# A two-layer decoder in fp32: VectorE makes the sums of the weights one item earlier in chunks of seven block products, and the block sums move to other buffers

## The chip, the cores and the metric

The kernel runs on one core of one Trainium2 chip. The metric is the time of one launch on the device in microseconds (us), lower is better. The kernel before was timed three times: 2167.9 us median, 2167.6 lowest, 2168.16 highest.

## What is computed

The reference is a decoder of two layers on 256 tokens of width 2048, all in fp32: a gated token mixer and a convolutional feed-forward part in layer 0, attention with forget gates and the same feed-forward part in layer 1, and a final norm. The change touches only the down projection of the feed-forward part, a product of a 256 x 5632 matrix with a 5632 x 2048 weight, once in each layer:

```python
def conv_ffn(xn, w_up, conv_w, conv_b, w_down):
    S = xn.shape[1]
    h = xn @ w_up
    hp = jnp.pad(h, ((0, 0), (CONV_W - 1, 0), (0, 0)))
    h = sum(hp[:, k:k + S] * conv_w[k] for k in range(CONV_W)) + conv_b
    gate, val = jnp.split(h, 2, axis=-1)
    return (jax.nn.silu(gate) * val) @ w_down
...
for l in range(DEPTH):
    ...
    h = h + conv_ffn(rmsnorm(h, f_norm[l]), f_w_up[l], f_conv_w[l],
                     f_conv_b[l], f_w_down[l])
```

## The kernel before

**Two parts of every number.** Each fp32 operand is split into a rounded part (`hi`, in a buffer `whi`) and a remainder (`lo`, in `wlo`), and TensorE multiplies hi by hi, hi by lo and lo by hi. For weights that arrive from memory, ScalarE (ACT in the profile) rounds (`whi`), and VectorE (DVE) then subtracts to get the remainder (`wlo`). So each piece of the weights costs one instruction on each of the two engines, and then 24 matmuls of 256 columns.

**The stream of items.** All weights pass through one `Stream`. Its items are pieces of 128 x 1024 numbers. At step i, `Stream.run` issues the load of item i + 6 on SyncE's queue (SP), splits item i + 3 into two parts, lets TensorE multiply item i, and then advances every piece of side work that is pending by one `yield`. Each engine works its own list strictly in this order. There are four buffers for loaded pieces (`raw`), four for rounded parts and four for remainders. A load waits until the piece that lay in its buffer has been split, and a rounded part is written once TensorE has done with the item four places back.

**Chunks of seven block products.** In the down projection (`seven_block`) the output is made in blocks of 512 columns: three in layer 0 (its last 512 columns are made in another way), four in layer 1. A block has 22 chunks of the weight. Most are plain, 24 matmuls. The chunks listed in `SUMMED` are done with seven block products instead of eight, from sums of weight blocks and sums of activation blocks. Such a chunk is two items of the stream: the first (`mult_plain`) multiplies three quarters of the loaded weights as they are, 9 matmuls; the second (`mult_sums`) has no load of its own, and multiplies four sums of weight blocks, 12 matmuls. In what follows a plain item is called C, the first item of a chunk of seven A, and the second B. A block runs as a sequence like C A B C A B C C A B. `order_of` sets it: two A B pairs in block 0, eight in the other blocks but the last of layer 1, which has six. Together that is 42 pairs.

**The sums of the weights.** `weight_sums` makes the four sums of a chunk with three additions on VectorE (lines 495, 497, 498). They lie in a buffer called `room`, of which there are two. In the kernel before, they are made when item A is split, so VectorE's list reads: the additions of A, the remainder of A, the remainder of B, the remainder of the next C, and so on. ScalarE rounds B from those sums, and VectorE then makes B's remainder from that.

**Side work.** The sums of the activations for the chunks of seven (`all_sums`, lines 474 to 484) are made at the start of a down projection and use the same two `room` buffers. At the end of a block's chunks of seven, the sums that TensorE has gathered in `m` are added to the result: in layer 1 by `sums_into_residual` (lines 590 to 602), which holds a `room` buffer (`one`) through five steps; in layer 0 by `sums_apart` (lines 611 to 631), which has its own buffer, and then turns each half of the block on VectorE (line 927), sends it to memory in four DMAs on SP's queue (line 934), fetches it back in another layout (line 938), and adds it to `h` (line 642). These DMAs stand in the same queue as the loads of the weights.

Of the kernel before, what the change touches and what calls it, by code (L numbers as in the profile page):

```python
# [14 lines left out]
OP = mybir.AluOpType  # L15
AX = mybir.AxisListType

P = 128
# [26 lines left out]
class Stream:  # L45
# [4 lines left out]
        self.items, self.pending = [], []  # L50
        self.raw, self.parts = {}, {}

    def chunk(self, src, mult, at, at_load=None, at_split=None, rows=(1, 1), place=None, split=None):


        self.items.append((src, mult, at_load, at_split, at, rows, place, split))

    def then(self, at_load=None, at_split=None, at_mult=None):
        self.items.append((None, at_mult, at_load, at_split, 0, None, None, None))

    def start(self, gen):
        self.pending.append(gen)
# [4 lines left out]
                self.pending.remove(g)  # L67

    def _load(self, i):
        src, _, at_load, _, _, _, place, _ = self.items[i]  # L70
        if at_load:
            at_load()
        if src is None:
            return
        if place is None:
            place = self.pool.tile([P, CHUNK], F32, name="raw", tag="raw", bufs=LOADS - AHEAD + 1)
        raw = place[:, :src.shape[1]]
        self.nc.sync.dma_start(raw, src)
        self.raw[i] = raw
# [10 lines left out]
        return hi, lo  # L90

    def _split(self, i):
        if self.items[i][3]:
            self.items[i][3]()
        raw, split = self.raw.pop(i, None), self.items[i][7]
        if split:
            self.parts[i] = split(raw)
            return
        if raw is None:
            return  # L100
        at, (n, pitch) = self.items[i][4:6]
        hi, lo = self.room(at)
        raw = raw.rearrange("p (n w) -> p n w", n=n)
        h, l = hi, lo
        if n > 1:
            h, l = (a[:, :n * pitch].rearrange("p (n w) -> p n w", n=n) for a in (h, l))
        else:
            h, l = h[:, None, :], l[:, None, :]
        h, l = (a[:, :, :raw.shape[2]] for a in (h, l))
        self.nc.scalar.activation(h, raw, AF.Copy)  # L110
        self.nc.vector.tensor_tensor(l, raw, h.bitcast(F32), op=OP.subtract)  # L111
        self.parts[i] = (hi, lo)
# [63 lines left out]
def build(ctx, tc, d, out):  # L176
# [307 lines left out]
        nc.vector.tensor_tensor(lo, f, hi.bitcast(F32), op=OP.subtract)  # L484

    def all_sums():
        for _ in range(4):
            yield
        for q in range(0, len(SUMMED), 2):
            yield from sums_of_blocks(q, SUMMED[q])  # L490
# [10 lines left out]
    def seven_block(blk, src, order, done, sums_done):  # L501
# [50 lines left out]
        def seven(c, i, first):  # L552
            q = SUMMED.index(c)
            sums = block_sums()[:, q]
            own = {}

            def split(raw):
                own["t"] = weight_sums(raw)
                return s.two_parts(raw[:, T:], TOK_AT)

            def mult_plain(hi, lo):
                if first:
                    box["m"] = main_ps()
                m, ps = box["m"], box["ps"]
                three(m[:, 0, :T], (hi, lo), at(2 * c, 0), 0, first, i == lasts)
                three(ps(0, T), (hi, lo), at(2 * c + 1, 0), 2, False, False)
                three(ps(0, 0), (hi, lo), [sums[:, 3, l, :] for l in range(2)], 1, False, False)

            def mult_sums(hi, lo):
                m, ps = box["m"], box["ps"]  # L570
                three(m[:, 1, :T], (hi, lo), [sums[:, 1, l, :] for l in range(2)], 0, first, i == lasts)
                three(m[:, 1, T:], (hi, lo), [sums[:, 0, l, :] for l in range(2)], 1, False, i == lasts)
                three(m[:, 0, T:], (hi, lo), [sums[:, 2, l, :] for l in range(2)], 2, False, i == lasts)
                three(ps(1, T), (hi, lo), at(2 * c + 1, 1), 3, False, False)
                if i == lasts:
                    s.start(sums_done(m))

            s.chunk(src[c], mult_plain, TOK_AT, split=split)
            s.chunk(None, mult_sums, TOK_AT, split=lambda _: s.two_parts(own["t"], TOK_AT))

        for i, (c, s7) in enumerate(order):
# [5 lines left out]
    def sums_into_residual(blk):  # L587

        def done(m):
            hh = by_token()[:, :, blk * 512:(blk + 1) * 512]  # L590
            one = room()[:, :3 * T].rearrange("p (a b) -> p a b", a=3)
            nc.scalar.activation(one[:, 0, :], m[:, 0, :T], AF.Copy)
            yield
            nc.vector.tensor_tensor(one[:, 1, :], one[:, 0, :], m[:, 0, T:], op=OP.add)
            nc.vector.tensor_tensor(one[:, 2, :], one[:, 1, :], m[:, 1, T:], op=OP.subtract)
            yield
            nc.vector.tensor_tensor(hh[:, :, :T], hh[:, :, :T], m[:, 1:, :T].to_broadcast([P, 2, T]), op=OP.add)
            yield
            nc.vector.tensor_tensor(hh[:, :, :T], hh[:, :, :T], one[:, 1:, :], op=OP.subtract)
            yield  # L600
            nc.vector.tensor_tensor(hh[:, :, T:], hh[:, :, T:], one[:, 0::2, :], op=OP.add)
            state["summed"] += 1
        return done

# [273 lines left out]
    def room():  # L878
        return ph.temp("room", [P, CHUNK])
# [419 lines left out]
```

## Time and profile before

| | |
|---|---|
| median of three runs | 2167.9 us |
| the profiled execution, its own time | 2168.81 us |
| its span, first to last instruction | 2167.1 us |
| mean granted TensorE clock | 0.999 |
| VectorE busy in the span | 1619.4 us, 75% |
| ScalarE busy in the span | 1187.0 us, 55% |
| DMA, mean | 208 GB/s |

The profile is of one execution. Its span runs from the first to the last instruction, and its own time is 1.7 us longer than the span. A row of a timeline gives the start in us from the start of the span, the duration in us, the engine, the line, the operation, what it writes and reads, and how many instructions of a kind stand together; in brackets, for how long the engine was idle before, and who ended that wait. In the views of waits the three numbers are us in total, how many times, and the longest. Two plain-looking things need care. A matmul's end is modelled, so TensorE (PE) that looks busy is only known to start its matmuls one after the other. And the busy share of VectorE is a mean over the whole span: in the chunks of seven it is far higher than in the plain ones.

### The profile page before, as it was taken

To read this page: it belongs to the slowest core of one execution; us is meant where nothing else is said; L and a number is where in the kernel's file an instruction comes from. 1 tells how busy PE (TensorE), PEld (TensorE's weight loads), DVE (VectorE), ACT (ScalarE), POOL (GpSimd) and SP (SyncE) were. 2 spreads that over 40 slices of the span, in tenths; PEclk is the share of its full clock that TensorE was granted. 3 is DMA by queue.
4 is the path that set the end of the run, shared out by engine and by line. 5 is a ranking of instruction groups with operands and counts; after the bars stand their busy time and mean duration, and the time that the engine had idled before them with its cause. 6 is when DMAs were issued, how large, how long until landed. Compare 5 with 4: busy or idle time off the path is not lost.

```text
span 2167.1 us, 45152 instructions
## 1 busy us (share of the span) xinstructions
PE 2157.8 (100%) x18594; PEld 2141.2 (99%) x18594; DVE 1619.4 (75%) x2335; ACT 1187.0 (55%) x1591; POOL 26.4 (1%) x46
## 2 busy tenths in 40 slices
PE   9999999999999999999999999999999999999998
PEld 9999999999999999999999999999999999999998
DVE  6696687777777688876777676668777777779887
ACT  6664455555555555554545665446555555555554
POOL 0000000000000000000001200000000000000000
PEclk9999999999999999999999999999999999999999
DMA  8686566666666567776778776567766666665665
GB/s 313 192 240 202 193 199 194 191 197 192 197 195 195 177 199 225 221 229 192 237 236 265 234 224 197 184 224 219 244 193 193 194 195 194 195 192 180 204 204 166
DMA packets 157551, 450.47 MB, mean 208 GB/s; under 512 B 26064, under 2 KB 48352, under 8 KB 156960
## 3 DMA queue, kind: packets, MB, share of 16 engines
q1 hardware_dynamic: 155808, 443.63, 65.9%
q0 software_dynamic: 1072, 3.41, 0.6%
q8 instruction: 145, 2.38, 0.4%
q14 instruction: 62, 0.51, 0.1%
q10 hardware_dynamic: 464, 0.55, 0.1%
HBM read 432.29 MB, written 15.22 MB: 207 GB/s over the span
## 4 chain that ended last, share of the span: by engine, by line
PE 100%; DVE 0%; ACT 0%; POOL 0%; issue 0%; DVEq 0%; POOLq 0%
PE ps L211 97%; PE mp L211 1%; PE mp L1149 0%; PE mp L756 0%; PE ps L1143 0%; PE ps L1144 0%; PE ps L1142 0%; PE mp L1148 0%; DVE h L723 0%; PE mp L406 0%; ACT sq L435 0%; DVE h L434 0%; DVE h L717 0%; ACT fin_t L709 0%; POOL ident L1185 0%
## 5 line engine op out<-in xcount | busy, mean ns | idle before, releaser
L111 DVE TENSOR_TENSOR wlo<-raw,whi 128x1024 fp32r<-128x1024 f32 (+1 forms) x736 | 893.6, 1220 | 295.9 <-ACT whi L110 292.7
L110 ACT ACTIVATE whi<-raw 128x1024 fp32r<-128x1024 f32 (+1 forms) x736 | 773.8, 1057 | 598.6 <-PE ps L211 500.8
L211 PE MATMUL ps<-X,whi 128*128 128x256 f32 (+1 forms) x6476 | 824.0, 279 | 0.0
L211 PEld LDWEIGHTS ps<-X,whi 128*128 128x128 f32 x6476 | 776.2, 188 | 6.5
L211 PE MATMUL ps<-X,wlo 128*128 128x256 f32 x3328 | 445.3, 276 | 0.0
L211 PEld LDWEIGHTS ps<-X,wlo 128*128 128x128 f32 x3328 | 409.8, 188 | 1.6
L211 PE MATMUL ps<-whi,ffn_H 128*128 128x256 f32 (+1 forms) x1892 | 308.8, 277 | 0.0
L211 PEld LDWEIGHTS ps<-whi,ffn_H 128*128 128x128 f32 x1892 | 260.4, 188 | 0.7
L211 PE MATMUL ps<-whi,X 128*128 128x256 f32 (+1 forms) x1336 | 221.3, 279 | 0.0
L211 PE MATMUL ps<-wlo,ffn_H 128*128 128x256 f32 (+1 forms) x944 | 195.3, 277 | 0.0
L211 PEld LDWEIGHTS ps<-whi,X 128*128 128x128 f32 x1336 | 187.1, 188 | 1.3
L898 DVE SCALAR_TENSOR_TENSOR ffn_room<-ffn_room,col 128x255 f32<-128x255 f32 x352 | 161.9, 481 | 6.4
L211 PE MATMUL ps<-whi,att_X 128*128 128x256 f32 (+2 forms) x970 | 164.3, 285 | 0.0
L211 PEld LDWEIGHTS ps<-wlo,ffn_H 128*128 128x128 f32 x944 | 146.9, 188 | 0.2
L211 PE MATMUL ps<-wlo,X 128*128 128x256 f32 (+1 forms) x666 | 144.4, 279 | 0.0
L387 DVE TENSOR_TENSOR ffn_room<-ps,rB 128x512 f32<-128x512 f32 x76 | 52.5, 691 | 119.1 <-PE ps L211 119.1
L211 PEld LDWEIGHTS ps<-whi,att_X 128*128 128x128 f32 x970 | 135.3, 188 | 3.5
L894 ACT ACTIVATE ffn_room<-ffn_room,col 128x256 f32<-128x256 f32 x176 | 96.3, 594 | 50.0 <-DVE ffn_room L387 50.0
L211 PEld LDWEIGHTS ps<-wlo,X 128*128 128x128 f32 x666 | 106.3, 188 | 0.5 <-DVE wlo L89 0.2
L211 PE MATMUL ps<-wlo,att_X 128*128 128x256 f32 (+2 forms) x476 | 105.4, 286 | 0.0
L88 ACT ACTIVATE whi<-ffn_room 128x1024 fp32r<-128x1024 f32 x42 | 44.7, 1064 | 64.9 <-DVE ffn_room L498 56.1
L211 PEld LDWEIGHTS ps<-wlo,att_X 128*128 128x128 f32 x476 | 75.4, 188 | 1.0
(216 smaller groups left out, 1609.3 us busy)
## 6 DMA issues: line engine op xcount, KB each, us to landing
raw<-up SPq DMA_DIRECT2D x352, 512.0 KB, 4.1
raw<-down SPq DMA_DIRECT2D x154, 512.0 KB, 4.3
raw<-a_in_u SPq DMA_DIRECT2D x32, 512.0 KB, 4.4
raw<-a_out SPq DMA_DIRECT2D x32, 512.0 KB, 4.0
raw<-b_q SPq DMA_DIRECT2D x32, 512.0 KB, 4.5
raw<-kvf_v SPq DMA_DIRECT2D x32, 512.0 KB, 4.9
raw<-b_g SPq DMA_DIRECT2D x32, 512.0 KB, 4.5
raw<-b_out SPq DMA_DIRECT2D x32, 512.0 KB, 4.2
```

The lines of the kernel that those rows point to most:

```text
L88: self.nc.scalar.activation(hi[:, :n], src, AF.Copy)
L110: self.nc.scalar.activation(h, raw, AF.Copy)
L111: self.nc.vector.tensor_tensor(l, raw, h.bitcast(F32), op=OP.subtract)
L211: nc.tensor.matmul(o, a, b, start=start, stop=stop, skip_group_check=True)
L387: nc.vector.tensor_tensor(a, src, rB[:, None, :].to_broadcast([P, 2, T]), op=OP.mult)
L894: nc.scalar.activation(c[:, m, :], a[:, m, :], AF.Identity, scale=w[2], bias=column(C_CONVB + l * 2 * KF + f))
L898: nc.vector.scalar_tensor_tensor(c[:, m, n:], a[:, m, :T - n], w[k], c[:, m, n:], op0=OP.mult, op1=OP.add)
```

## The change

Four things are changed.

- An item of the stream may carry a function `early`. `_split(i)` calls that of item i + 1 first, so that it runs ahead of all that the split of item i issues.
- A's three additions become such an `early`: they stand on VectorE ahead of the remainder of the item before A.
- `all_sums` waits three steps instead of four before it begins, since a `room` buffer is now wanted one item sooner.
- `sums_into_residual` no longer takes a `room` buffer. It uses two buffers called `turned`, which in layer 1 are free at that time, and a quarter that two steps read from one buffer is now copied by ScalarE into the second.

```diff
     def _split(self, i):
+        if i + 1 in self.raw and self.items[i + 1][8]:
+            self.items[i + 1][8](self.raw[i + 1])
         if self.items[i][3]:
             self.items[i][3]()
...
     def all_sums():
-        for _ in range(4):
+        for _ in range(3):
             yield
...
-            def split(raw):
+            def early(raw):
                 own["t"] = weight_sums(raw)
-                return s.two_parts(raw[:, T:], TOK_AT)
...
-            s.chunk(src[c], mult_plain, TOK_AT, split=split)
+            s.chunk(src[c], mult_plain, TOK_AT, split=lambda raw: s.two_parts(raw[:, T:], TOK_AT), early=early)
...
-            one = room()[:, :3 * T].rearrange("p (a b) -> p a b", a=3)
-            nc.scalar.activation(one[:, 0, :], m[:, 0, :T], AF.Copy)
-            yield
-            nc.vector.tensor_tensor(one[:, 1, :], one[:, 0, :], m[:, 0, T:], op=OP.add)
-            nc.vector.tensor_tensor(one[:, 2, :], one[:, 1, :], m[:, 1, T:], op=OP.subtract)
-            yield
+            left, right = (ph.temp("turned", [P, 512]).rearrange("p (a b) -> p a b", a=2) for _ in range(2))
+            nc.scalar.activation(right[:, 0, :], m[:, 0, :T], AF.Copy)
+            yield
+            nc.vector.tensor_tensor(left[:, 0, :], right[:, 0, :], m[:, 0, T:], op=OP.add)
+            nc.vector.tensor_tensor(left[:, 1, :], left[:, 0, :], m[:, 1, T:], op=OP.subtract)
+            yield
+            nc.scalar.activation(right[:, 1, :], left[:, 1, :], AF.Copy)
             nc.vector.tensor_tensor(hh[:, :, :T], hh[:, :, :T], m[:, 1:, :T].to_broadcast([P, 2, T]), op=OP.add)
             yield
-            nc.vector.tensor_tensor(hh[:, :, :T], hh[:, :, :T], one[:, 1:, :], op=OP.subtract)
-            yield
-            nc.vector.tensor_tensor(hh[:, :, T:], hh[:, :, T:], one[:, 0::2, :], op=OP.add)
+            nc.vector.tensor_tensor(hh[:, :, :T], hh[:, :, :T], left, op=OP.subtract)
+            yield
+            nc.vector.tensor_tensor(hh[:, :, T:], hh[:, :, T:], right, op=OP.add)
```

TensorE's list of matmuls is the same in both kernels, instruction by instruction. SyncE's list is the same too, apart from the names of buffers. What moves is on VectorE. The first place is in block 1 of layer 0, behind that block's second turned half; the rows are VectorE's list there in the kernel before, with the buffers' numbers (a row with `raw` and `whi` of 1024 is the remainder of a C, one of 768 that of an A, one that reads `room` and `whi` that of a B).

```order
L495 TENSOR_TENSOR ffn0_room_10152<-raw_10080 128x512
L497 TENSOR_TENSOR ffn0_room_10152<-raw_10080,ffn0_room_10152 128x256
L498 TENSOR_TENSOR ffn0_room_10152<-raw_10080,ffn0_room_10152 128x256
L89 TENSOR_TENSOR wlo_10157<-raw_10080,whi_10156 128x768
L89 TENSOR_TENSOR wlo_10173<-ffn0_room_10152,whi_10172 128x1024
L111 TENSOR_TENSOR wlo_10203<-raw_10133,whi_10202 128x1024
L495 TENSOR_TENSOR ffn0_room_10234<-raw_10150 128x512
L497 TENSOR_TENSOR ffn0_room_10234<-raw_10150,ffn0_room_10234 128x256
L498 TENSOR_TENSOR ffn0_room_10234<-raw_10150,ffn0_room_10234 128x256
L89 TENSOR_TENSOR wlo_10239<-raw_10150,whi_10238 128x768
L89 TENSOR_TENSOR wlo_10254<-ffn0_room_10234,whi_10253 128x1024
```

And the same place in the changed kernel, where the lines are numbered two higher from line 92 on:

```order
L113 TENSOR_TENSOR wlo_10140<-raw_10063,whi_10139 128x1024
L89 TENSOR_TENSOR wlo_10157<-raw_10080,whi_10156 128x768
L89 TENSOR_TENSOR wlo_10173<-ffn0_room_10135,whi_10172 128x1024
L497 TENSOR_TENSOR ffn0_room_10202<-raw_10154 128x512
L499 TENSOR_TENSOR ffn0_room_10202<-raw_10154,ffn0_room_10202 128x256
L500 TENSOR_TENSOR ffn0_room_10202<-raw_10154,ffn0_room_10202 128x256
L113 TENSOR_TENSOR wlo_10207<-raw_10133,whi_10206 128x1024
L89 TENSOR_TENSOR wlo_10239<-raw_10154,whi_10238 128x768
L89 TENSOR_TENSOR wlo_10254<-ffn0_room_10202,whi_10253 128x1024
```

The three additions of the second A, which read its load (`raw_10150` before, `raw_10154` now), stood behind the remainder of the C before it (`wlo_10203`) and now stand ahead of it (`wlo_10207`), so that this remainder is queued behind the landing of A's load. In block 2 of layer 0 the list has the same shape at the same place.

The second place is in ScalarE's list in layer 1, where a block's sums are added to the residual. The rows are those of the kernel before:

```order
L110 ACTIVATE whi_25267<-raw_25204 128x1024
L592 ACTIVATE ffn1_room_25283<-ps_24708 128x256
L110 ACTIVATE whi_25287<-raw_25222 128x1024
L88 ACTIVATE whi_25323<-raw_25252 128x768
L88 ACTIVATE whi_25352<-ffn1_room_25319 128x1024
```

And in the changed kernel:

```order
L112 ACTIVATE whi_25269<-raw_25206 128x1024
L593 ACTIVATE ffn1_turned_25286<-ps_24710 128x256
L112 ACTIVATE whi_25294<-raw_25224 128x1024
L88 ACTIVATE whi_25326<-raw_25254 128x768
L598 ACTIVATE ffn1_turned_25286<-ffn1_turned_25285 128x256
L88 ACTIVATE whi_25356<-ffn1_room_25290 128x1024
```

The copy from `m` goes to another buffer, and two steps later one copy of 128 x 256 between two of the `turned` buffers is added, four times in the kernel, once for each block of layer 1.

More of the change, by code (lines that the diff above doesn't have):

```diff
@@ L51, in __init__, with chunk @@
         self.raw, self.parts = {}, {}
-    def chunk(self, src, mult, at, at_load=None, at_split=None, rows=(1, 1), place=None, split=None):
-        self.items.append((src, mult, at_load, at_split, at, rows, place, split))
+    def chunk(self, src, mult, at, at_load=None, at_split=None, rows=(1, 1), place=None, split=None, early=None):
+        self.items.append((src, mult, at_load, at_split, at, rows, place, split, early))
     def then(self, at_load=None, at_split=None, at_mult=None):
-        self.items.append((None, at_mult, at_load, at_split, 0, None, None, None))
+        self.items.append((None, at_mult, at_load, at_split, 0, None, None, None, None))
     def start(self, gen):
@@ L69, in _load @@
     def _load(self, i):
-        src, _, at_load, _, _, _, place, _ = self.items[i]
+        src, _, at_load, _, _, _, place, _, _ = self.items[i]
         if at_load:
```

## The prediction

> **What bounds the kernel now.** I read the page first: its list of engines, then the chain that ended last, then the views of waits of TensorE and of its weight loads.
>
> ```profile
> PE 2157.8 (100%) x18594; PEld 2141.2 (99%) x18594; DVE 1619.4 (75%) x2335; ACT 1187.0 (55%) x1591; POOL 26.4 (1%) x46
> ...
> PE 100%; DVE 0%; ACT 0%; POOL 0%; issue 0%; DVEq 0%; POOLq 0%
> ```
>
> ```profile
> PE mp L756 <- POOL ident L1185: 1.5, 1, 1.5
> ...
> PEld ps L211 <- DVE wlo L89: 0.2, 1, 0.2
> ```
>
> TensorE is busy for 2157.8 of 2167.1 us, and in the whole program it waited 1.5 us at the start and its weight loads 0.2 us, once, for a remainder of VectorE's. The other 7.6 us lie behind the last matmul. The chain shows that end:
>
> ```profile
> 2153.59 5.67 PE mp L211 x48
> 2159.26 0.02 issue
> ...
> 2161.92 0.79 DVE h L723 x2
> ```
>
> So there is nothing in the middle to gain but 0.2 us. The list of matmuls stays the same, and a change on VectorE can only move the time by making TensorE wait, or by ending that one wait. The question is what the new order makes late.
>
> **What the change frees, and why that is not on the path.** The waits inside the down projection of layer 1 (2 x 8 + 6 + 2 = 24 pairs) show what the early sums remove:
>
> ```profile
> ACT whi L88 <- DVE ffn_room L498: 35.2, 21, 2.8
> DVE wlo L89 <- ACT whi L88: 7.8, 22, 0.5
> ```
>
> ScalarE waited 35.2 us for the third addition, and VectorE 7.8 us for ScalarE's rounding of B, 0.34 us a time. With the sums made earlier both waits go. But nobody on TensorE stands behind them, but for the 0.2 us. The gain is 0.2 us, once.
>
> **The cost in layer 0: a load that lands late.** Here is VectorE in block 1, at the place of the first pair of lists, and TensorE's first use of the remainder of that C (the second of the rows of VectorE).
>
> ```profile
> 828.35 1.23 DVE L89 TENSOR_TENSOR wlo<-ffn_room,whi 128x1024 fp32r<-128x1024 f32 x1 [0.34 <-ACT whi L88]
> 829.73 1.22 DVE L111 TENSOR_TENSOR wlo<-raw,whi 128x1024 fp32r<-128x1024 f32 x1 [0.16 <-ACT whi L110]
> 831.90 0.69 DVE L495 TENSOR_TENSOR ffn_room<-raw 128x512 f32<-128x512 f32 x1 [0.94 <-DMA raw<-down]
> 832.63 0.43 DVE L497 TENSOR_TENSOR ffn_room<-raw,ffn_room 128x256 f32<-128x256 f32 x1
> 833.09 0.42 DVE L498 TENSOR_TENSOR ffn_room<-raw,ffn_room 128x256 f32<-128x256 f32 x1
> 833.43 0.95 DVE L89 TENSOR_TENSOR wlo<-raw,whi 128x768 fp32r<-128x768 f32 x1
> ```
>
> ```profile
> 833.47 0.39 PE L211 MATMUL ps<-wlo,ffn_H 128*128 128x256 f32 x2
> ```
>
> Before, the remainder of C ended at 830.95, 2.5 us ahead of its use at 833.47. Then VectorE stood idle for 0.94 us, until A's load landed at 831.9. In the new order the additions come first, and C's remainder is queued behind that landing. The additions start at 831.90 and the next instruction follows them at 833.43, so they cost 1.53 us; C's remainder then takes 1.22 us and ends at 834.65. TensorE wants it at 833.47: it **waits 1.2 us**. Whether VectorE gets there a few tenths sooner by the waits that went does not matter, since the start is pinned by the landing.
>
> Is the landing itself moved? SP's queue tells what it hangs on:
>
> ```profile
> 822.57 1.78 SPq L934 DMA_DIRECT2D way_d<-ffn_turned  x4
> 824.45 0.39 SPq L78 DMA_DIRECT2D raw<-down  x1
> 824.89 0.45 SPq L938 DMA_DIRECT2D ffn_drows<-way_d  x1
> 825.44 0.85 SPq L78 DMA_DIRECT2D raw<-down  x2
> ```
>
> ```profile
> 821.84 0.70 DVE L927 STREAM_TRANSPOSE ffn_turned<-ffn_apart 128x512 f32<-128x512 f32 x1
> ```
>
> A's load is the first of the two at 825.44. It was issued behind four DMAs that wait for the turned half (VectorE, 821.84 to 822.54), C's load, and one fetch; and it took 6.4 us to land. The turning stands behind the same instructions in both orders, since the additions that were moved ahead of one remainder stood ahead of it anyway. So I take the landing as it is. The bounds come from all such loads between 815 and 900 us:
>
> ```profile
> DMA to landing us min/median/max: 3.5/4.5/7.2
> ```
>
> At 3.5 us it lands at 828.9; the additions then start no sooner than B's remainder of 828.35 lets them (829.5), C's remainder ends by 832.3, and there is no wait. At 7.2 us it lands at 832.6 and the wait is 2.0 us. I take the row of this very load, 1.2 us.
>
> In block 2 the same happens, in the same shape (the first of the two loads is A's, 6.2 us to its landing):
>
> ```profile
> 882.53 0.85 SPq L78 DMA_DIRECT2D raw<-down  x2
> ```
>
> ```profile
> 886.76 1.23 DVE L111 TENSOR_TENSOR wlo<-raw,whi 128x1024 fp32r<-128x1024 f32 x1
> 888.72 0.69 DVE L495 TENSOR_TENSOR ffn_room<-raw 128x512 f32<-128x512 f32 x1 [0.73 <-DMA raw<-down]
> ...
> 890.25 0.95 DVE L89 TENSOR_TENSOR wlo<-raw,whi 128x768 fp32r<-128x768 f32 x1
> ```
>
> ```profile
> 890.59 0.39 PE L211 MATMUL ps<-wlo,ffn_H 128*128 128x256 f32 x2
> ```
>
> C's remainder would start at 890.25 and end at 891.48, TensorE wants it at 890.59: **0.9 us**, between 0 and 1.9 by the same bounds of the landing. Block 0 has no turned halves in the queue at its pairs, so it has no such wait.
>
> **What comes behind these waits.** The load of the A after next in block 1 goes into the buffer that C's late remainder reads, so it is issued when that ends. Its old issue, and the use of the remainder that it will hold up:
>
> ```profile
> 830.98 0.33 SPq L78 DMA_DIRECT2D raw<-down  x1
> ```
>
> ```profile
> 841.29 0.39 PE L211 MATMUL ps<-wlo,ffn_H 128*128 128x256 f32 x2
> ```
>
> It moves from 830.98 to 834.7 and lands, at 3.5 to 4.5 us, at 838.2 to 839.2. Additions and remainder (1.53 + 1.22) end by 842.0 at the latest; TensorE, itself 1.2 us late, asks at 842.5. At 5 us and over there would be another few tenths. I take 0, and 0.3 for each block into the range.
>
> **Layer 1.** No halves are turned there, so the loads aren't held up. The danger is another: C's remainder is queued behind 1.53 us of additions at a place where VectorE has little lead. The tightest stretch of block 1:
>
> ```profile
> 1989.35 1.23 DVE L111 TENSOR_TENSOR wlo<-raw,whi 128x1024 fp32r<-128x1024 f32 x1 [0.89 <-ACT whi L110]
> ...
> 1994.63 1.22 DVE L89 TENSOR_TENSOR wlo<-ffn_room,whi 128x1024 fp32r<-128x1024 f32 x1 [0.34 <-ACT whi L88]
> ...
> 1998.80 1.23 DVE L111 TENSOR_TENSOR wlo<-raw,whi 128x1024 fp32r<-128x1024 f32 x1 [0.61 <-ACT whi L110]
> ...
> 2003.36 1.22 DVE L89 TENSOR_TENSOR wlo<-ffn_room,whi 128x1024 fp32r<-128x1024 f32 x1 [0.34 <-ACT whi L88]
> 2004.51 1.22 DVE L111 TENSOR_TENSOR wlo<-raw,whi 128x1024 fp32r<-128x1024 f32 x1
> ```
>
> ```profile
> 2006.26 0.39 PE L211 MATMUL ps<-wlo,ffn_H 128*128 128x256 f32 x2
> ```
>
> The C of the last row ended at 2005.73, 0.53 us ahead of its use. Now 1.53 us of additions stand ahead of it, but four idle times go: 0.89 and 0.61 us are just where additions now stand, ahead of a remainder that waits for ScalarE, and twice 0.34 us is the wait for B's rounding. Together 2.18 us. So C would end at 2005.73 + 1.53 - 2.18 = 2005.1, sooner than before. If none of the idle time were filled, it would end at 2007.26 and TensorE would wait 1.0 us, in each of blocks 1 to 3. I take 0, the end near the rows, and keep 3.0 us as the other end.
>
> **The other edits.** The copy that ScalarE makes in addition costs what the one from `m` cost, four times:
>
> ```profile
> L592 ACT ACTIVATE ffn_room<-ps x4: 359/384/384, 1979.8 to 2139.1; 128x256 f32<-128x256 f32 x4
> ```
>
> That is 1.5 us of an engine that is 55% busy. It waits for a subtraction on VectorE, and the rounding of the next item is queued behind it; but that subtraction stands ahead of the remainder whose rounding ScalarE has just made, so it is done by then. If it were not, the price would be at most those 0.4 us each of a rounding that VectorE waits for. `all_sums` begins one item sooner, at plain items. Both at nothing.
>
> **The sum.** 1.2 + 0.9 - 0.2 = **+1.9 us**, and a few tenths for what follows the waits: +2.1. The profiled execution itself took 2168.8 us (its span of 2167.1 and 1.7 around it), which would become 2170.9. It was 0.9 slower than the median of the runs, 2167.9, to which I put the same step: **2170.0 us**. That is 0.1%; a measurement of this kernel can tell about 0.2% (4.3 us) from no change, so this counts as no change.
>
> **The rivals.**
>
> *The loads land sooner and nobody waits.* For it: the two landings of 6.4 us and 6.2 us are single events in one execution, and the median is 4.5. Against it: both blocks show the same, behind the same fetch and four DMAs of the turned half. Then only the 0.2 us are left: 2167.7 us. Chance 0.28.
>
> *VectorE falls behind in layer 1 too.* It decides where the idle times are not filled, because a load or a rounding is late. 2.1 + 3 x 1.0 gives 2173.0 us, slower by over 0.2%. Against it are the 2.18 us above. Chance 0.03.
>
> *TensorE's clock falls.* The rows of the end show when it does:
>
> ```profile
> 2158.00:2162.80 4.80, 1.24 (x11) 1.04 (x9) 3.81 (x14) 1.81 (x6) 0.00 (x0) 1.00 0.48 182
> 2162.80:2167.10 4.30, 0.00 (x0) 0.00 (x0) 0.00 (x0) 0.00 (x0) 0.00 (x0) 0.50 0.64 242
> ```
>
> TensorE's work ended at 2159.26, and its granted clock is 1.00 until 2162.8 and 0.50 behind it: 3.5 us of idleness. A wait over 3.5 us in block 1 would cost itself and, if the clock then stays at half for as long as it took to fall (an estimate), another 1.8 us. That makes 2167.9 + 3.5 + 1.8 + 0.9 = 2174.1 us or more. It begins where A's load lands 2.3 us later than it did. Chance 0.02. The Trainium skill has this as a rule (TensorE: Matmul & The Clock Gate, "Why this matters for your kernels"): leave no gap over some 3 us between matmuls, or the clock goes back to half. By that rule too, gaps of 1.2 us cost only themselves. The trace agrees with it, at 3.5 us.
>
> *Faster by over 0.2%* would need 4.3 us off TensorE's own work or off the end behind the last matmul, neither of which the change touches: 0.01, at some 2163.
>
> **How the numbers follow.** The forecast has 0.66, with its own range of 2168.6 to 2172.0. The range to hold 8 in 10 takes in the rival without waits below, 2167.4, and above the larger landings (2.0 + 1.9 + 0.6 - 0.2): 2172.2. Faster 0.01; within 0.2%, forecast and first rival, 0.94; slower, the second and third, 0.05.
>
> **What would show it.** In the changed profile TensorE's waits should list the remainder of a C (line 113), some 1.2 us in block 1 and 0.9 in block 2 of layer 0, and VectorE's first addition (line 497) should wait for loads some 3 us longer there. ScalarE's waits for the third addition (line 500) should almost be gone. If TensorE waits nowhere, the landing was sooner; if it waits in layer 1, the idle times were not filled.

## The result, and the profile after

The changed kernel takes 2176.18 us (median of six runs, 2171.5 to 2178.68), the kernel before on the same chip 2168.03 us (six runs, 2167.55 to 2169.13). The ratio is 1.0036, with a 95% interval of 1.0023 to 1.0049. So it is **slower by 0.36%**, some 8 us. The forecast was 2170.0 us, and its range ended at 2172.2.

The profiled execution took 2175.67 us, 6.9 more than that of the kernel before; its span is 6.8 longer. These are the page's list of engines and its chain that ended last:

```profile
PE 2163.2 (100%) x18594; PEld 2146.3 (99%) x18594; DVE 1619.4 (74%) x2335; ACT 1191.7 (55%) x1595; POOL 26.4 (1%) x46
...
PE 98%; DVE 1%; DMA 1%; issue 0%; ACT 0%; POOL 0%; DVEq 0%; ACTq 0%; POOLq 0%
```

The same 18594 matmuls take 5.4 us longer. VectorE's work has the same sum, and a load and VectorE have come into the chain. The waits of TensorE, of its weight loads and of VectorE's additions in the changed kernel:

```profile
PE ps L213 <- DVE wlo L113: 1.4, 1, 1.4
```

```profile
PEld ps L213 <- DVE wlo L113: 1.8, 2, 1.6
```

```profile
DVE ffn_room L497 <- DMA raw<-down: 9.9, 9, 2.6
```

All of TensorE's waits for VectorE that are listed sum to under 2 us. They cannot make 6.8. Where the rest lies is seen by counting matmuls in stretches of 50 us. In a row of this view stand the stretch, its length, then for each engine the busy us and in brackets how many instructions started, then the granted clock. First the kernel before, then the changed one:

```profile
800.00:850.00 50.00, 50.00 (x443) 50.00 (x442) 45.25 (x58) 26.23 (x28) 0.00 (x0) 1.00 0.68 221
...
2050.00:2100.00 50.00, 50.00 (x444) 50.00 (x443) 44.08 (x57) 27.14 (x31) 0.00 (x0) 1.00 0.69 209
```

```profile
800.00:850.00 50.00, 48.58 (x426) 48.19 (x425) 42.44 (x55) 26.08 (x27) 0.00 (x0) 1.00 0.65 208
...
2050.00:2100.00 50.00, 50.00 (x427) 50.00 (x427) 41.77 (x52) 27.66 (x31) 0.00 (x0) 1.00 0.60 191
```

The last row of the changed kernel is the finding. TensorE is fully busy there, waits for nothing, has a granted clock of 1.00, and yet makes 427 matmuls in 50 us in place of 443 or 444; it does so in every stretch from 2000 us to its end. Its mean matmul of 256 columns is 281 ns in place of 276, and they start 117.7 ns apart in place of 113.4. This slow pace begins at one instruction, and the view of TensorE's weight loads has it (two rows of the changed kernel, around 2000.7 us):

```profile
2000.27 0.41 PEld L213 LDWEIGHTS ps<-whi,ffn_H 128*128 128x128 f32 x3
2000.72 0.30 PEld L213 LDWEIGHTS ps<-wlo,ffn_H 128*128 128x128 f32 x2
```

Three loads from 2000.27 on, at 0.113 us each, would put the next at 2000.61; it starts at 2000.72. It is the first load of the remainder of a C, which VectorE finished at 2000.67. That is 0.11 us, too short to be listed as a wait. From there to the last matmul, 165.1 us later, the pace stays slow: 165.1 x (1 - 427/443) = 5.96 us.

The kernel before has such a stretch too, 39.8 us up to its last matmul, and it begins at the one wait of 0.2 us that its profile listed:

```profile
2118.68 0.30 PEld L211 LDWEIGHTS ps<-whi,X 128*128 128x128 f32 x2
2119.17 0.19 PEld L211 LDWEIGHTS ps<-wlo,X 128*128 128x128 f32 x1 [0.18 <-DVE wlo L89]
```

That cost it 39.8 x 16/443 = 1.44 us. So the two profiles differ by the 17 matmuls missing between 800 and 850 us (17 x 0.113 = 1.9 us), by 0.1 us at 2000.7, and by 5.96 - 1.44 = 4.5 us of slow pace: 6.5 of the 6.8 us. The rest, 0.3 us, lies in the first 8 us, where nothing was changed and the profiled executions differ by some tenths of a us.

Why VectorE was late there is told by its rows in the changed kernel:

```profile
1984.59 0.69 DVE L497 TENSOR_TENSOR ffn_room<-raw 128x512 f32<-128x512 f32 x1 [1.17 <-DMA raw<-down]
...
1997.11 1.23 DVE L89 TENSOR_TENSOR wlo<-ffn_room,whi 128x1024 fp32r<-128x1024 f32 x1 [0.88 <-ACT whi L88]
...
1999.45 1.22 DVE L113 TENSOR_TENSOR wlo<-raw,whi 128x1024 fp32r<-128x1024 f32 x1
```

In the kernel before, the same remainder and its first weight load are these two rows:

```profile
1996.98 1.22 DVE L111 TENSOR_TENSOR wlo<-raw,whi 128x1024 fp32r<-128x1024 f32 x1
```

```profile
1998.33 0.30 PEld L211 LDWEIGHTS ps<-wlo,ffn_H 128*128 128x128 f32 x2
```

It ended at 1998.20, 0.13 us ahead of that load. The C that the forecast took for the tightest of the block, two plain items later in VectorE's list, had 0.4 us. Of the 2.18 us of idle time that the forecast wanted to fill, 0.89 and 0.34 us lie ahead of this remainder. They are gone from their old places, but two others have come, 1.17 us for a load that an addition, being earlier, now finds not landed, and 0.88 us for a rounding: 2.05 us in place of 1.23. VectorE's row stands 2.47 us later than before and the time at which TensorE wants it 2.28 us later, and that uses up the 0.13 us.

The 0.88 us come about on ScalarE. B's rounding is queued there behind a square, which waits for a step of VectorE's own side work (line 448), and that step now stands behind the additions and the remainder of a C:

```profile
1995.40 0.64 ACT L450 ACTIVATE sq<-h 128x512 f32<-128x512 f32 x1 [1.29 <-DVE h L448]
```

The wait of VectorE for B's rounding in layer 1 is not gone but doubled, as the view of waits shows for the same stretch in which it was 7.8 us before:

```profile
DVE wlo L89 <- ACT whi L88: 15.6, 20, 1.6
...
ACT whi L88 <- DVE ffn_room L500: 2.4, 3, 1.8
```

Layer 0 holds the other surprise. VectorE in block 1 before (the two turned halves, of which the second was shown above) and after:

```profile
810.06 0.41 DVE L614 TENSOR_TENSOR ffn_apart<-ffn_apart,ps 128x256 f32<-128x256 f32 x1
...
810.85 0.69 DVE L495 TENSOR_TENSOR ffn_room<-raw 128x512 f32<-128x512 f32 x1
...
815.76 0.70 DVE L927 STREAM_TRANSPOSE ffn_turned<-ffn_apart 128x512 f32<-128x512 f32 x1
```

```profile
810.83 0.69 DVE L497 TENSOR_TENSOR ffn_room<-raw 128x512 f32<-128x512 f32 x1 [2.19 <-DMA raw<-down]
...
813.49 0.41 DVE L616 TENSOR_TENSOR ffn_apart<-ffn_apart,ps 128x256 f32<-128x256 f32 x1
...
817.67 0.71 DVE L929 STREAM_TRANSPOSE ffn_turned<-ffn_apart 128x512 f32<-128x512 f32 x1
...
823.53 0.70 DVE L929 STREAM_TRANSPOSE ffn_turned<-ffn_apart 128x512 f32<-128x512 f32 x1
...
832.84 0.69 DVE L497 TENSOR_TENSOR ffn_room<-raw 128x512 f32<-128x512 f32 x1 [2.60 <-DMA raw<-down]
...
834.37 1.22 DVE L113 TENSOR_TENSOR wlo<-raw,whi 128x1024 fp32r<-128x1024 f32 x1
```

And SP's queue in the changed kernel, at the place shown of before:

```profile
824.26 1.78 SPq L936 DMA_DIRECT2D way_d<-ffn_turned  x4
826.14 0.39 SPq L78 DMA_DIRECT2D raw<-down  x1
826.57 0.45 SPq L940 DMA_DIRECT2D ffn_drows<-way_d  x1
827.12 1.73 SPq L78 DMA_DIRECT2D raw<-down  x2
```

At the first pair of the block the addition, brought ahead, waits 2.19 us for its load. Before, VectorE made a C's remainder and two steps of the last block's sums in that time. Now those sums (line 616, line 614 before) start at 813.49 in place of 810.06, both turned halves come 1.7 to 1.9 us later (0.3 of it from the start of the program), the four stores of the second on SP start at 824.26 in place of 822.57, and the loads behind them in SP's queue are issued 1.7 us later. At 832.84 the additions of the pair whose order the change section lists wait for such a load, C's remainder is queued behind it, and TensorE waits 1.6 us.

### The profile page after: what moved, and what is told of

It is laid out like the page before. It is cut to its first block, busy times and chain, and to the rows that moved or that the text cites. A ratio compares the mean times of both kernels' runs of the same rounds, so it can differ in the third digit from the quotient of the medians.

```text
span 2173.9 us, 45157 instructions
## 1 busy us (share of the span) xinstructions
PE 2163.2 (100%) x18594; PEld 2146.3 (99%) x18594; DVE 1619.4 (74%) x2335; ACT 1191.7 (55%) x1595; POOL 26.4 (1%) x46
## 4 chain that ended last, share of the span: by engine, by line
PE 98%; DVE 1%; DMA 1%; issue 0%; ACT 0%; POOL 0%; DVEq 0%; ACTq 0%; POOLq 0%
PE ps L213 96%; PE mp L213 1%; DMA raw<-down 1%; PE mp L1151 0%; DVE wlo L113 0%; PE mp L758 0%; PE ps L1145 0%; PE ps L1146 0%; PE ps L1144 0%; PE mp L1150 0%; DVE ffn_room L497 0%; DVE wlo L89 0%; DVE ffn_room L499 0%; ACT whi L88 0%; DVE h L725 0%
## 5 line engine op out<-in xcount | busy, mean ns | idle before, releaser
L310 ACT ACTIVATE X<-h,col 128x256 fp32r<-128x256 f32 x64 | 29.8, 499 | 62.6 <-DVE h L395 57.8
```

The lines of the kernel that those rows point to most:

```text
L310: nc.scalar.activation(dst[:, kt, :T], h[:, kt, :], AF.Copy, scale=g)
```

## The experiments

Every time is a median with its range. Each ratio is to the kernel before on the same chip in the same hours: 2168.08 us (29 runs) for e1 to e4, 2167.75 us (28 runs) for e5 to e8, 2168.25 us (33 runs) for e9 to e12. The theories:

- A: TensorE has two paces. A weight load that comes a little late can put it into the slower one, where it stays until 512-column matmuls come, or until it recovers by itself. In the seven-product part of layer 1 none come.
- B: the new buffers and the additional copies disturb TensorE.
- C: all of it comes from the late loads of layer 0.
- D (formed after e8): the loss of layer 0 starts at the first pair of a block, by the chain of stores and loads above.

### One part of the change at a time: e1, e2, e3

All three keep the new buffers, the copies and the earlier `all_sums`. A rule says for which chunks the additions are brought ahead; for the others they are made at their old place.

```diff
+def EARLY(layer, blk, nth):
+    return layer == 0        # e1;  e2: layer == 1;  e3: False
...
-            s.chunk(src[c], mult_plain, TOK_AT, split=lambda raw: s.two_parts(raw[:, T:], TOK_AT), early=early)
+            s.chunk(src[c], mult_plain, TOK_AT, split=split, early=early if ahead else None)
```

> The changed kernel, with the additions ahead of the preceding remainder in layer 0 alone; in layer 1 they stand where they stood before, with the new buffers. Theory A (a wait in layer 1, however short, leaves TensorE at some 117.7 ns a matmul instead of 113.4 until the end; in layer 0 TensorE waits for late loads and recovers): TensorE waits some 1.8 us in blocks 1 and 2 of layer 0, its pace changes only near 2120 us as before, and the time is 2168.0 + 1.8 = 2169.8 us. Theory B (the new buffers and the additional copy of layer 1 crowd TensorE's reads and so slow its pace there): the slow pace of the changed kernel, from about 2000 us on, is here too, and the time is about 2175.

> The changed kernel, with the additions ahead of the preceding remainder in layer 1 alone. Theory A: no wait in layer 0; in layer 1 the remainder of a C in block 1 is late by about 0.1 us near 1999 us, and from there TensorE runs at 117.7 ns: 2168.0 + 4.6 = 2172.6 us, with a wide spread over the runs (some 2168 to 2177), as it depends on whether and when the pace comes back. Theory C (all of the loss comes from the loads in layer 0): 2168.

> The changed kernel with the additions back at their old place in both layers; the new buffers, the additional copies and the earlier start of the activations' sums stay. Theory A: the time of the kernel before, 2168.0, with a slow pace only near the end. Theory B: slow pace from about 2000 us, some 2173.

| | us | range, runs | ratio to before, interval |
|---|---|---|---|
| before | 2168.08 | 2166.77 to 2170.01, 29 | |
| e1, layer 0 alone | 2170.09 | 2168.91 to 2172.83, 11 | 1.0011, 1.0002 to 1.0020 |
| e2, layer 1 alone | 2173.30 | 2168.63 to 2174.58, 11 | 1.0020, 1.0011 to 1.0029 |
| e3, neither | 2167.55 | 2167.05 to 2168.49, 11 | 0.9997, 0.9988 to 1.0007 |

e3 costs nothing: B falls. Layer 0 gives 2.0 us and layer 1 gives 5.2, together 7.2 of the 8.1 us: C falls too. e2 is the telling one, since its profile lists no wait of TensorE or its weight loads for VectorE at all. Its rows of weight loads and two stretches:

```profile
2005.72 0.41 PEld L217 LDWEIGHTS ps<-whi,ffn_H 128*128 128x128 f32 x3
2006.13 0.30 PEld L217 LDWEIGHTS ps<-wlo,ffn_H 128*128 128x128 f32 x2
```

```profile
1950.00:2000.00 50.00, 50.00 (x442) 49.96 (x442) 43.85 (x56) 26.64 (x32) 0.00 (x0) 1.00 0.57 182
...
2050.00:2100.00 50.00, 50.00 (x427) 50.00 (x427) 41.76 (x52) 28.21 (x32) 0.00 (x0) 1.00 0.62 198
```

The fourth load starts 0.41 us behind the first, in place of 3 x 0.113 = 0.34: it is 0.07 us late. Behind it TensorE makes 427 matmuls in 50 us for the 157 us to the end. It is the remainder of the very C that the forecast had worked out. The remainder that is late in the changed kernel is late here too, by 0.12 us at 1998.2, and there the faster pace came back after some six matmuls. The eleven times of e2 lie in two groups, three from 2168.6 to 2169.3 and eight from 2172.9 to 2174.6, and nothing between.

### A remainder held up in the kernel before: e4

```diff
+            def held_up(raw):
+                t = ph.temp("turned", [P, 512])
+                nc.vector.tensor_tensor(t, raw[:, :512], raw[:, 512:], op=OP.add)
+                for _ in range(11 - 1):
+                    nc.vector.tensor_tensor(t, t, raw[:, 512:], op=OP.add)
+                return s.two_parts(raw, TOK_AT)
```

This stands ahead of one remainder in block 0 of layer 1.

> The kernel before, with one remainder of a plain chunk in block 0 of layer 1 (the eighth chunk, near 1946 us) held up by eleven additions of 128 x 512 ahead of it on VectorE, 7.9 us of work into a buffer that nobody reads, so that TensorE waits once for about half a us. Nothing is early. Theory A: if the pace doesn't come back by itself, TensorE runs at 117.7 instead of 113.4 ns from there to the end, 215 us instead of 38, which costs 6.5 us and the wait itself: 2175.0 us. If it comes back within some matmuls, as after the waits of layer 0: 2168.5. Theory B (a wait costs itself alone): 2168.5 in every run.

(The "theory B" of this text is not the B of the list above: it says that a wait costs itself and no more.)

Measured: 2174.14 us (2173.16 to 2174.76, seven runs), ratio 1.0028 (1.0018 to 1.0039). The total agrees with theory A, but by accident. The eleven additions also held up `all_sums` behind them, and several items came late:

```profile
PEld ps L211 <- DVE wlo L89: 3.2, 4, 2.1
```

```profile
1950.00:2000.00 50.00, 47.85 (x395) 47.25 (x394) 44.15 (x55) 24.37 (x27) 0.00 (x0) 0.97 0.60 184
2000.00:2050.00 50.00, 50.00 (x444) 50.00 (x443) 44.05 (x56) 27.06 (x32) 0.00 (x0) 1.00 0.67 209
```

The slow pace lasted from 1957.5 to 1978.4 us, 21 us, and ended, without 512-column matmuls, at two further late loads, of which the second waited 2.06 us:

```profile
1983.30 0.19 PEld L211 LDWEIGHTS ps<-wlo,ffn_H 128*128 128x128 f32 x1 [2.06 <-DVE wlo L89]
```

Behind this wait the granted clock was 0.5 for 3.4 us, from 1983.7 to 1987.1, and the matmuls started 213 ns apart, which is the 0.97 in the row of this stretch and some 1.6 us of the time. Then the faster pace was back. So the time is made of waits, a slow stretch and a fall of the clock together. This run tells nothing for or against A, except that A has to allow for a slow stretch that ends at a longer wait. A smaller disturbance was needed.

### One addition, one late load: e5, e6, e12

e5 is e3 with one addition of 128 x 256 ahead of one remainder in block 1 of layer 1, which had 0.24 us to spare. e6 is e5 with ten 512-column matmuls in the plain chunk behind it. e12 is e5 again.

```diff
+            def held_up(raw):
+                nc.vector.tensor_tensor(ph.keep("spot", [P, T]), raw[:, :T], raw[:, T:2 * T], op=OP.add)
+                return s.two_parts(raw, TOK_AT)
...
-            s.chunk(src[c], mult, TOK_AT)
+            s.chunk(src[c], mult, TOK_AT, split=held_up if layer and blk == 1 and i == 5 else None)
...
+                    if layer and blk == 1 and i == 6:   # e6 alone
+                        between()
                     left = wide_next()
```

> The kernel of e3 (no additions brought forward, 2167.55 us, no slow stretch in layer 1) with one extra addition of 128x256 ahead of one remainder of C: that of the second chunk behind a pair in block 1 of layer 1, used near 1998 us, which was ready only 0.24 us before its use. The addition (estimate 0.4 us, from 0.69 us for the 128x512 one) makes it 0.1 to 0.2 us late, once, with no load and no other queue concerned. Theory A (a weight load that is a little late puts TensorE from 113.4 to 117.7 ns a matmul until 512-wide ones come, and in layer 1 none come): waits of PE and PEld sum to under 0.6 us, a slow stretch from about 1998 us to the end (some 160 us), and about 160 x 4.3/117.7 = 5.8 us more: 2173.5 us, or a mixture of 2167.6 and 2173.5 where the late load does not always tip it. Rival (a wait costs itself): 2167.6 to 2168.2, no slow stretch.

> e5 with the same late remainder, and ten 512-column matmuls in the plain chunk behind it (each takes 6 ns longer than two of 256, 0.06 us in all). Theory A: the slow stretch ends there, within 5 us of its start: 2167.55 + 0.2 + 0.06 + 0.2 = 2168.0 us, and fast matmuls to the end. Rival (the lateness itself moved the later work, and the slow stretch is a consequence of what comes late afterwards): the slow stretch starts again behind the wide ones, and the time stays where e5 is, 2173 to 2174.

> e5 once more, for a profile: its eleven times fell into two groups (2166.9 to 2169.4, five; 2173.2 to 2174.4, six), and the profiled one was of the lower group, with a wait of 0.2 us and no slow stretch behind it. Theory A: a profile of the upper group shows the same wait of about 0.2 us near 1998 us, then 117.7 ns a matmul to the end, and nothing else that is late; one of the lower group shows what e5 showed. Rival: the upper group has more waits, of PE, PEld or a load, summing to 5 us.

| | us | range, runs | runs over 2171 |
|---|---|---|---|
| e5 | 2173.21 | 2166.91 to 2174.36, 11 | 6 |
| e12, the same kernel | 2169.57 | 2167.96 to 2174.41, 8 | 3 |
| e6, then wide | 2167.97 | 2166.87 to 2169.63, 11 | 0 |

The profiled execution of e5 took 2169.35 us, that of e12 2173.61. It is the same kernel, with the same late weight load. The weight loads of e5, then of e12:

```profile
1999.13 0.30 PEld L217 LDWEIGHTS ps<-wlo,ffn_H 128*128 128x128 f32 x2 [0.19 <-DVE wlo L93]
```

```profile
1998.68 0.30 PEld L217 LDWEIGHTS ps<-wlo,ffn_H 128*128 128x128 f32 x2 [0.19 <-DVE wlo L93]
```

The matmuls behind it, again e5 and then e12:

```profile
2000.16 0.62 PE L217 MATMUL ps<-whi,ffn_H 128*128 128x256 f32 x4
...
2000.85 0.62 PE L217 MATMUL ps<-whi,ffn_H 128*128 128x256 f32 x4
...
2001.53 0.62 PE L217 MATMUL ps<-whi,ffn_H 128*128 128x256 f32 x4
```

```profile
1999.73 0.64 PE L217 MATMUL ps<-whi,ffn_H 128*128 128x256 f32 x4
...
2000.44 0.63 PE L217 MATMUL ps<-whi,ffn_H 128*128 128x256 f32 x4
...
2001.14 0.63 PE L217 MATMUL ps<-whi,ffn_H 128*128 128x256 f32 x4
```

From row to row there are six matmuls (the two with `wlo` between are left out). In e5 the two steps take 0.69 and 0.68 us, 114 ns a matmul; in e12 0.71 and 0.70, 118 ns. The stretch from 2050 to 2100 us, again e5 and then e12:

```profile
2050.00:2100.00 50.00, 50.00 (x443) 50.00 (x442) 44.04 (x57) 27.88 (x33) 0.00 (x0) 1.00 0.67 207
```

```profile
2050.00:2100.00 50.00, 50.00 (x427) 50.00 (x426) 42.66 (x53) 28.24 (x32) 0.00 (x0) 1.00 0.63 194
```

In e5 the pace recovered after some six matmuls; in e12 it stayed slow for 165 us, to the end. Neither waits for anything else of note in layer 1 (e5's profile has a slow stretch of some 40 us at the very end, as the kernel before). So one lateness of a fifth of a microsecond costs 0.2 us in about half of the executions and 0.2 + 6.0 in the other half. With ten 512-column matmuls behind it, none of eleven executions is in the upper group, in place of nine of nineteen. That bears A out: what decides is the pace, and not what comes late afterwards. It rests on the times; in e6's profiled execution the pace had come back by itself 1.9 us ahead of the wide matmuls.

### The cure in layer 1: e11, and the changed kernel with it: e7

e7 is the changed kernel with ten 512-column matmuls in each of five plain chunks of blocks 1 and 2 of layer 1; e11 is e2 with the same.

```diff
+                    if layer and blk in (1, 2) and i % 5 == 0:
+                        between()
                     left = wide_next()
```

> The changed kernel with ten 512-column matmuls in each of five plain chunks of blocks 1 and 2 of layer 1 (10 x 0.06 = 0.6 us). Theory A: slow stretches in layer 1 last at most some 15 us each; what is left of the change is the waits of layer 0 (0.2 + 1.5 us) and 0.6 us: 2168.0 + 1.75 + 0.6 + up to 1 = 2170.3 to 2171.5 us, with less spread between executions than the 2171.5 to 2178.7 of the changed kernel. Rival (VectorE is late in layer 1 over and over, and each lateness costs): 2176.2 + 0.6 = 2176.8.

> e2 (early additions in layer 1 alone: 2173.3 us, with two groups of executions near 2168.8 and 2173.8) with ten 512-column matmuls in each of five plain chunks of blocks 1 and 2 of layer 1 (0.6 us in all). Theory A: no execution keeps a slow stretch from block 1 or 2 to the end; what can remain begins in block 3 (40 us, 1.4 us): 2168.2 to 2170.0, the upper group gone. Rival (the time of e2's upper group is VectorE being late again and again): 2173.3 + 0.6 = 2173.9.

e11 measured 2169.59 us (2168.88 to 2170.77, eleven runs; ratio 1.0005, 0.9996 to 1.0014): the upper group is gone, and what was 5.2 us above before is 1.3 us, of which some 0.6 is the price of the wide matmuls. As A expected.

e7 measured 2173.44 us (2169.84 to 2176.64, six runs; ratio 1.0027, 1.0015 to 1.0038), 2 us above what A expected, and its spread was not smaller. Its profiled execution (2173.78 us) shows why: layer 0 cost more this time, and the place that has no wide matmuls, block 3, was slow from 2125.7 us to the end (1.4 us).

```profile
PE ps L213 <- DVE wlo L113: 2.2, 2, 1.6
```

```profile
PEld ps L213 <- DVE wlo L113: 3.1, 4, 1.8
```

All but 0.2 us of these waits lie in layer 0. There is also a slow stretch in layer 0, 13 us of block 1 from 821.5 us on, which begins at a load 0.28 us late, ends at the wait of 1.8 us and costs 0.5 us. In blocks 1 and 2 of layer 1 no slow stretch shows, though that one late load is there, 0.24 us late, in the middle of eight wide matmuls. So the cure did what A says where it was put, and the size that I expected of the remainder was wrong: I had taken the loss of layer 0 from one profile, and it differs from execution to execution.

### The loss in layer 0: e8, e9, e10

By the forecast's step, only pairs whose C is queued behind a late load cost anything. e8 brings the additions ahead in layer 0 but not for the second and fourth pair of blocks 1 and 2, where that was seen. e9 spares the first pair of blocks 1 and 2 also. e10 brings them ahead for nothing but those two first pairs.

```diff
+def EARLY(layer, blk, nth):
+    return layer == 0 and (blk == 0 or nth not in (1, 3))                  # e8
+    return layer == 0 and (blk not in (1, 2) or nth not in (0, 1, 3))      # e9
+    return layer == 0 and blk in (1, 2) and nth == 0                       # e10
```

> Early additions in layer 0 alone (as e1, 2170.1 us), but not for the four chunks (two each in blocks 1 and 2) where e1 and the changed kernel have the addition waiting for its load ahead of C's remainder. Theory A (the loss of layer 0 is C's remainder queued behind the landing of the next load, at those chunks alone): no wait of PE over 0.1 us in layer 0, time that of e3, 2167.4 to 2168.0. Rival (bringing the additions forward in layer 0 costs wherever it stands): between 2168.8 and 2170.1, in proportion to the chunks left.

> Early additions in layer 0 alone as in e8 (2170.6 us), and in blocks 1 and 2 not for the first pair either (spared there: the first, second and fourth pairs). Theory D (the loss of layer 0 starts at the first pair of blocks 1 and 2: its addition, brought ahead, waits 2.1 us for its load with the partial sums of the block before queued behind it on VectorE; their transposes, the stores of the turned sums on SP and the loads behind those in SP's queue follow 1.5 to 2.5 us later, and these later loads are what C's remainders and the chunks' own remainders then wait for): the second way_d store starts as in e3, the load behind it lands near 831.6 us, no wait of PE over 0.1 us in layer 0, and 2167.4 to 2168.2 us. Rival (early additions cost anywhere in layer 0): still 2169 to 2170.

> Additions brought ahead for two chunks of the whole program only: the first pair of block 1 and of block 2 in layer 0. Theory D: these two are enough: the load behind the stores lands 1 to 2.5 us later than in e3, TensorE waits 0.5 to 2 us in block 1 and up to 1 us in block 2, in some executions a slow stretch follows; 2168.5 to 2171 us. Theory A alone in the form of e8 (only the pairs whose own C is queued behind the landing cost): 2167.4 to 2168.0, no wait.

| | us | range, runs | ratio to before, interval |
|---|---|---|---|
| e8, second and fourth spared | 2170.60 | 2167.69 to 2173.27, 10 | 1.0013, 1.0004 to 1.0022 |
| e9, first spared too | 2167.64 | 2166.68 to 2169.71, 11 | 0.9997, 0.9988 to 1.0006 |
| e10, first alone | 2169.92 | 2167.37 to 2172.43, 11 | 1.0007, 0.9999 to 1.0016 |

e8 is a miss: sparing the pairs that wait takes nothing away. Its rows of VectorE and of SP:

```profile
834.47 0.69 DVE L501 TENSOR_TENSOR ffn_room<-raw 128x512 f32<-128x512 f32 x1 [2.13 <-DMA raw<-down]
```

```profile
824.27 1.78 SPq L947 DMA_DIRECT2D way_d<-ffn_turned  x4
...
828.13 0.85 SPq L82 DMA_DIRECT2D raw<-down  x2
```

The additions are back at their old place, and still they wait 2.13 us, for a load that was issued at 828.13 (825.44 before) behind stores that started at 824.27. That led to theory D. In e9 the same rows read:

```profile
831.76 0.69 DVE L501 TENSOR_TENSOR ffn_room<-raw 128x512 f32<-128x512 f32 x1 [1.00 <-DMA raw<-down]
```

```profile
822.62 1.78 SPq L947 DMA_DIRECT2D way_d<-ffn_turned  x4
...
825.46 1.25 SPq L82 DMA_DIRECT2D raw<-down  x2
```

Everything is where it was before the change, no wait of TensorE for VectorE is listed, and the time is that of e3. So with its second and fourth pairs spared, the whole loss hangs on the first. e10, the first alone, has the second stores 1.2 us later than e9 (823.8 against 822.6) and a median 1.7 us above before, with an interval that still holds 1, so that the first pairs alone are not shown to cost anything; what shows them is e9 against e8. Its profiled execution shows only 0.4 us of it in layer 0. Its upper runs, like those of e1 and e8, are more than the listed waits can make. A slow stretch from block 1 to the next 512-column matmuls, which come near 928 us, would be of the size (93 us from 835 us on: 93 x 16/443 = 3.4 us). The profiles of e1, e8 and e10 show none, and that of e7 only the 13 us above, so for layer 0 this is argued and not shown.

None of these versions is faster than the kernel before by what can be told: e3 and e9 have 0.9997, with intervals that reach over 1.

## Why the prediction was wrong

- *TensorE sets the time, and the change can only make it wait.* Right for the bound. Wrong in the second half: it can also leave it at a slower pace, with no wait to be seen.
- *Layer 0, waits of 1.2 and 0.9 us.* The mechanism was right, a C queued behind the landing of the next A's load, and the sum nearly so: 1.9 us in the profile of the changed kernel, 2.0 us between the medians of e1 and before. That the sum came out is partly luck: in the changed kernel all of it lies in block 1, 1.9 us in place of 1.2, and block 2 has nothing in place of 0.9 (in e1's profile the weight loads wait 1.1 and 0.6 us in the two blocks). And one step of it failed, "so I take the landing as it is". The turning does stand behind the same instructions as before, but one of these, the first pair's addition, now waits 2.19 us for a load of its own that it used to find landed. I had looked at the order, and not for when each instruction's input is there. e8 and e9 show that this step carries the loss.
- *Layer 1, "I take 0".* **This is the step that failed**, in two ways. The first is the lead. The row that I called the tightest of block 1 was not: the C two plain items before it had 0.13 us to spare and not 0.4, and ahead of it 1.23 us of idle time went and 2.05 came, at other places. That made VectorE late by 0.11 us in the profile, nothing near the 1.0 us of the other end. The second, which has the size, is that the price of a lateness was taken as the lateness itself. e5 and e12 show that 0.2 us of it cost some 6.0 us more in half of the executions. e2, which is layer 1 alone, costs 5.2 us.
- *The gain of 0.2 us from the one wait in block 3.* The same fault in small: in the profile of before that wait was the start of 39.8 us at the slow pace, and so stood for 1.4 us. That fits with the profiled execution being 0.9 us above the median. I had noted this and not asked why.
- *The new buffers and copies at nothing.* Right: e3.
- *The rivals.* The place of the second was right (layer 1), with the wrong price (3 x 1.0 us) and so too small a chance. The clock did not fall in the changed kernel: it is 1.00 in every row of it, with waits of up to 1.6 us, and TensorE slowed by 3.6% with the clock at full. But the 3.5 us that I took from the end of the program as what it needs to fall are too many: in e4 it fell to half behind a wait of 2.06 us. I had put beside it a rule of the Trainium skill (TensorE: Matmul & The Clock Gate, "Why this matters for your kernels"), to leave no gap over some 3 us. The waits of up to 1.8 us here agree with it; e4's wait of 2.06 us, which should have been harmless by it, does not, and there the measurement decides.
- *What would show it.* ScalarE's waits for the third addition fell from 35.2 to 2.4 us, and VectorE's additions waited for loads, as said. The list had nothing on the pace of matmuls, which is where the time was.

## What to carry to other kernels

Where TensorE is busy for all of the span, count its matmuls in equal stretches of both profiles before looking at waits: a stretch with fewer matmuls and no wait is time that no list of waits will show. Judge an engine that feeds it by the least time to spare of its deliveries and not by its idle time, and when work is brought forward, ask of each instruction moved whether its input is there by then, and who stands in the queues behind it, other engines' DMAs too. Ten 512-column matmuls behind a place that is known to run late cost 0.06 us and, by e6 and e11, cap what a lateness can cost.

## What the runs showed of the hardware

- Back-to-back matmuls of 256 columns, each with its own weight load, run at one of two paces, 113.4 or 117.7 ns from start to start (443 or 427 in 50 us), at a granted clock of 1.00. A weight load that is 0.07 us late is enough to bring the slower one (e2).
- The slower pace can last for the rest of the program (165 us in e12), or go after six matmuls (e5), or end at a longer wait after 21 us (e4) or 13 us (e7). Ten matmuls of 512 columns (eight, some of 256, and two more) were always followed by the faster one in the runs with profiles here; eight alone were not (e9: 117.8 ns from 6.9 us to the next wide ones at 22 us). By the Trainium skill (TensorE: Matmul & The Clock Gate, "Back-to-back issue gap") the spacing in such a stream is set by the matmul and the weight load together. That fits with a weight load as the trigger, but why the same late load tips the pace in one execution and not in the next, no run here shows.
- A late load is not the only way in. Every profile here, of the kernel before too, has two more stretches at 117.8 ns, some 14 us from around 93 us and some 5.5 us from around 988 us, which begin where one product follows another, with no load more than 0.01 us late. The second ends where 512-column matmuls come. They are the same in all the kernels and take no part in the comparison.
- Behind a wait of TensorE of 2.06 us the granted clock was 0.5 for 3.4 us, with matmuls of 256 columns 213 ns apart (e4); behind waits of up to 1.8 us (e7) it stayed at 1.00. In e4 another wait, of 0.48 us, had ended 1.5 us before, and whether it had a part in it no run here shows.
- Executions of one kernel fell into two groups 5 to 6 us apart (e2, e5, e12). With a median of six runs, such a kernel's time depends on how many fall into each.
